# Joining two 256-column matmuls into one of 512 columns in seven-product (Strassen-type) layers of a diffusion block

## The chip, the cores and the metric

The kernel runs on one core of one Trainium2 chip. The metric is device time in microseconds (us) of one execution; lower is better. Five engines work side by side, each in the order of its own queue: TensorE (PE in the profile; its weight loads are shown as PEld), VectorE (DVE), ScalarE (ACT), GpSimd (POOL) and SyncE (SP). SP and POOL mainly issue DMAs here.

## The reference

One layer on 512 latent tokens of width 2048: modulated RMSNorm, attention and short-conv mixer, output projection, then a gated MLP with a depthwise convolution over tokens. All arithmetic is float32. What the change touches is the MLP:

```python
def conv_ffn(h, w_up, cw, cb, w_down):
    u = dwconv3(h @ w_up, cw, cb)          # 2048 -> 2 x 5504
    a, g = jnp.split(u, 2, axis=-1)
    return (a * jax.nn.silu(g)) @ w_down   # 5504 -> 2048

# x = x + gt_f * conv_ffn(hf_l, ...), then a final RMSNorm
```

## The kernel before

Tensors lie with features on the 128 partitions and the 512 tokens (T) along the columns; `HS` are the two halves H0 and H1 of 256 tokens. To keep float32 accuracy with the reduced-precision matmul type, every operand is split into a high part (a cast, on ACT) and a low part (operand minus cast, on DVE). A product then takes three matmuls: high weights by high data, high weights by low data, low weights by high data. `mm3` issues these three; each of the three loads its own 128x128 weights.

The up projection: the first three output tiles (six column groups) go row by row (`row`, over the 16 input tiles `hf`). For the other 40 tiles f a 2x2 scheme with seven products takes the place of eight: token halves and weight blocks are added and subtracted beforehand (`t_sums` makes the token sums T1, T2 and T4; `up_load` brings blocks 11, 12, 22 and sums s1 and s3, the sums by a second DMA that adds onto the first). The products run in the order p1 ("11"), p2 ("21"), then of the tile before q4 ("4") and q3 ("22"), then p6 ("2"), q5 ("1") and p7 ("3"). Each (`product`) splits a 128x1024 weight block (`split4`: u19p2h is the high part for product p2 of tile 19, u19p2l the low part; three buffers each) and calls `mm3` for eight input tiles into 256 columns of a PSUM bank. `u19a`, `u19b` and `u19c` are the three banks of tile 19. The results are put together on DVE into `cg` and `ca`, and `acts` applies convolution and gating; L1213 and L1214 form the weight sums in place on DVE (u_11 plus s1; u_12 plus that).

The activations of the last 36 tiles are paired; `pair_sums` makes seven operands of 256 columns per pair, high and low halves side by side in one tile of 512 columns (`tp`), which POOL's DMAs send to DRAM (`t_d`). The work of `pair_sums` is a generator in the queue `bg`; each `pump(1)` runs it up to its next `yield`, and `product` pumps once per product. Tiles of the pool `t2` hold the `tp` operands, the `hf` and the `T` tiles.

The down projection does seven tiles plainly (`d`, 512 columns), then 24 steps of seven products over a window of six pairs: operands come back from DRAM (`w<-t_d`, in the same side-by-side form), `weights_of` loads the blocks of a step and forms s3 on DVE (L1290), after which POOL's DMA adds a fourth block onto s1 (L1291), and L1351 and L1352 add s1 onward. `seven` runs a product, `into` adds its result onto the accumulators `c` (L1338 in steps 8 and later). `v19q4l` is the low part of the weights for product q4 of step 19. From step 16 on sums of squares for the final norm (`ssq`, L347) run on DVE too.

The order of instructions on each engine is set by a scheduler when the program is built, from the code's order and its own time estimates; the engines then run their queues in that order.

Of the kernel before, what the change touches and what calls it, by code (L numbers as in the profile page):

```python
# [72 lines left out]
def block_kernel(ctx, tc, xt, ctxt, ctxn, c, c_ctx, w_ada, small, w_in, w_inc, w_q, w_kv, w_out,  # L73
# [65 lines left out]
    nth = {"raw": 0, "w": 0}  # L139
# [45 lines left out]
    def mm3(ps, w, x, first, last, on_top=False):  # L185
        with tc.issue_after(behind.pop()) if behind else ExitStack():
            PE.matmul(ps, w[0], x[0], start=first, stop=False, skip_group_check=on_top)  # L187
        PE.matmul(ps, w[0], x[1], start=False, stop=False, skip_group_check=on_top)  # L188
        PE.matmul(ps, w[1], x[0], start=False, stop=last, skip_group_check=on_top)  # L189

# [740 lines left out]
    def hf_tile(j, cols=slice(0, T)):  # L931
        if j not in hf:
# [7 lines left out]
        hi, lo = (z[:, cols] for z in hf[j])  # L940
        A.copy(out=hi, in_=xr)
        ins = V.tensor_tensor(out=lo, in0=xr, in1=hi.bitcast(F32), op=ALU.subtract)
        hf_last[:] = hf_last[1], ins.ins
# [91 lines left out]
    def pair_sums(p, e, o):  # L1035
# [4 lines left out]
        def put(n, src):  # L1040
            z = t2([P, T], F32R, f"tp{p}{n}")
            A.copy(out=z[:, :256], in_=src)  # L1042
            V.tensor_tensor(out=z[:, 256:], in0=src, in1=z[:, :256].bitcast(F32), op=ALU.subtract)  # L1043
            G_.dma_start(t_d[p, OPS.index(n)], z.bitcast(F32))  # L1044
# [30 lines left out]
    def t_sums(j):  # L1075

        e, o = xres[2 * j], xres[2 * j + 1]
        i, c = j // 2, HS[j % 2]
        if j % 2 == 0:
            for n in (1, 2, 4):  # L1080
                TT[n, i] = tuple(t2([P, T], F32R, f"T{n}{i}{z}") for z in "hl")

        def put(dst, src):
            hi, lo = dst
            A.copy(out=hi, in_=src)
            V.tensor_tensor(out=lo, in0=src, in1=hi.bitcast(F32), op=ALU.subtract)

        V.tensor_tensor(out=e[:, H0], in0=e[:, H0], in1=e[:, H1], op=ALU.subtract)
        V.tensor_tensor(out=e[:, H1], in0=o[:, H1], in1=e[:, H1], op=ALU.subtract)
        put(half_of(hf[2 * j], 1), e[:, H1])  # L1090
        V.scalar_tensor_tensor(out=o[:, H1], in0=e[:, H0], scalar=-1.0, in1=o[:, H1], op0=ALU.mult, op1=ALU.subtract)
        V.scalar_tensor_tensor(out=o[:, H0], in0=o[:, H1], scalar=-1.0, in1=o[:, H0], op0=ALU.mult, op1=ALU.subtract)
        for n, src in ((1, e[:, H0]), (2, o[:, H1]), (4, o[:, H0])):
            put(tuple(z[:, c] for z in TT[n, i]), src)

    def operand(n, j):
        if n in ("11", "3"):
            return half_of(hf[2 * j], n == "3")
        if n in ("21", "22"):
            return half_of(hf[2 * j + 1], n == "22")  # L1100
        return half_of(TT[int(n), j // 2], j % 2)
# [21 lines left out]

    pss = [bank_of(i, f"uf{g}") for g, i in enumerate((2, 3, 4, 5, 1, 0))]
# [3 lines left out]
    for k in range(EARLY):  # L1128
        row(pss, held[k], hf[k], k, H0)
        pump(1)  # L1130
    drain()
    for k in range(EARLY):
        hf_tile(k, H1)
        row(pss, held[k], hf[k], k, H1)
# [12 lines left out]
    for k in range(EARLY, NK):  # L1147
# [7 lines left out]
        row(pss, w, hf[k], k)  # L1155
# [21 lines left out]
    def finish(st):  # L1177
        f, a22, s4, u2, u3, pa, pc, cg, ca = st
        product(pa, a22, "4", f"u{f}q4", False)
        A.activation(ca[:, H0], pa[:, :256], AF.Identity, scale=-1.0)  # L1180
        product(pc, s4, "22", f"u{f}q3", False)
        V.tensor_tensor(out=cg[:, H1], in0=pc[:, :256], in1=u2, op=ALU.add)  # L1182
        acts(f, cg, ca)
# [15 lines left out]
    for f in range(G // 2, NF):  # L1199
# [8 lines left out]
        ca = cp.tile([P, T], F32, tag="ca", bufs=2, name=f"ca{f}")  # L1208
# [3 lines left out]
        V.tensor_tensor(out=cg[:, H0], in0=pb[:, :256], in1=u1, op=ALU.add)  # L1212
        V.tensor_tensor(out=a11, in0=a11, in1=s1, op=ALU.add)  # L1213
# [105 lines left out]
    def seven(z, ps, a, n, nm, first, pump_at=()):  # L1319
# [11 lines left out]
    def into(z, i, cols, ps, minus=False):  # L1331

        o = acc2[z.m + i][:, cols]
        if z.st < 8:
            ins = V.tensor_tensor(out=o, in0=o, in1=ps[:, :256], op=ALU.subtract if minus else ALU.add)
        else:
            g = ng[:, z.m + i:z.m + i + 1] if minus else mod[:, 80 + z.m + i:81 + z.m + i]
            ins = V.scalar_tensor_tensor(out=o, in0=ps[:, :256], scalar=g, in1=o, op0=ALU.mult, op1=ALU.add)  # L1338
# [255 lines left out]
```

## Time and profile before

| | |
|---|---|
| runs | 2155.0, 2151.49, 2147.65 us; median 2151.49 |
| profiled execution | 2158.83 us, span 2157.0 us, clock 0.994 |
| up projection, seven products | about 884 to 1695 us of the span |
| plain part of down | about 1697 to 1770 us |
| 24 steps of down | about 1770 to 2145 us |

The columns of the views: in the timeline, start, duration, engine, line, operation, output<-inputs, partitions x elements, and in brackets the idle time before the instruction with what ended it. Durations overlap a little: an engine starts its next instruction before the last one's end, so the distance between starts is what a queue of instructions costs. In the table of windows each engine has its busy time and its number of instructions.

### The profile page before, as it was taken

The page shows a single profiled execution, that of the slowest core. Times are in us where ns is not written, and L with a number is a line of the kernel's source. Part 1 is how long each engine was busy: PE and PEld are TensorE (multiplying, and loading weights), DVE is VectorE, ACT ScalarE, POOL GpSimd, SP SyncE. Part 2 cuts the span into 40 slices and gives each one's busy share as a digit, 9 for nine tenths or more (in the row PEclk, how much of TensorE's full clock was granted, in tenths as well). Part 3 has the DMA queues.
Part 4 walks back from the last instruction along what each step waited for, and adds up shares of the span by engine and source line. Part 5 has one row for each costly group of instructions (what it writes and reads, how often), then busy time and mean ns, then how long its engine had stood idle before and what let it go on. Part 6 is the DMA issues. An engine that isn't in the chain of part 4 may idle for free.

```text
span 2157.0 us, 37744 instructions
## 1 busy us (share of the span) xinstructions
PE 2104.9 (98%) x14458; PEld 1946.7 (90%) x14458; DVE 1769.0 (82%) x2859; ACT 1047.1 (49%) x1710; POOL 188.1 (9%) x270
## 2 busy tenths in 40 slices
PE   7899999999999999999999999999999999999997
PEld 4688788888888888999999999999999889999997
DVE  7998987778886889788888788788888658888877
ACT  5533333555552237555555555555555333333445
POOL 0000000000000000111211111111111000000000
PEclk9999999999999999999999999999999999999998
DMA  9979785334559986577887877877887999877683
GB/s 335 345 275 337 270 279 176 128 126 162 177 199 348 344 278 192 159 217 201 241 232 215 240 229 220 237 231 219 241 229 218 341 335 290 254 220 236 196 247 111
DMA packets 162121, 513.89 MB, mean 238 GB/s; under 512 B 18962, under 2 KB 23314, under 8 KB 156306
## 3 DMA queue, kind: packets, MB, share of 16 engines
q1 hardware_dynamic: 133364, 418.14, 56.5%
q0 software_dynamic: 27488, 92.29, 18.3%
q8 instruction: 113, 1.85, 0.3%
q10 hardware_dynamic: 1088, 1.05, 0.1%
q14 instruction: 68, 0.56, 0.1%
HBM read 464.22 MB, written 46.14 MB: 237 GB/s over the span
## 4 chain that ended last, share of the span: by engine, by line
PE 86%; DVE 6%; DMA 5%; issue 1%; ACT 1%; SPq 0%; DVEq 0%; POOLq 0%; ACTq 0%
PE pp L187 4%; PE pp L189 4%; PE pp L188 4%; PE o L189 1%; PE o L187 1%; PE o L188 1%; DMA ada<-in_w_ada 1%; PE d L187 1%; PE d L189 1%; PE d L188 1%; PE uf L187 1%; PE uf L188 1%; PE of L187 1%; PE of L188 1%; PE of L189 1%
## 5 line engine op out<-in xcount | busy, mean ns | idle before, releaser
L1044 POOL DMA_DIRECT2D t_d<-tp x126 | 71.9, 574 | 468.3 <-DVE tp L1043 465.4
L255 DVE SCALAR_TENSOR_TENSOR ada<-ada,sv 128x1024 f32<-128x1024 f32 x68 | 82.1, 1219 | 12.1 <-DMA ada<-in_w_ada 12.0
L166 ACT CAST w_0h<-rw 128x512 fp32r<-128x512 f32 (+1 forms) x63 | 38.3, 618 | 108.3 <-PE pp L188 63.1
L1121 POOL DMA_DIRECT2D u_s<-in_w_up x80 | 70.2, 878 | 224.4 <-DMA u_s<-in_w_up 131.5
L233 DVE SCALAR_TENSOR_TENSOR ada<-ada,sv 128x1024 f32<-128x1024 f32 x64 | 77.5, 1217 | 4.4 <-DMA ada<-in_w_ada 3.9
L522 DVE SCALAR_TENSOR_TENSOR ada<-ada,svc 128x1024 f32<-128x1024 f32 x64 | 76.0, 1220 | 2.3 <-DMA ada<-in_w_ada 2.3
L785 POOL TENSOR_TENSOR gr<-gr,half 128x8 f32<-128x8 f32 x4 | 10.1, 2524 | 628.7 <-DVE gr L784 536.8
L1042 ACT CAST tp<-a 128x256 fp32r<-128x256 f32 x90 | 34.7, 405 | 60.5 <-DMA t_d<-tp 54.1
L167 DVE TENSOR_TENSOR w_0l<-rw,w_0h 128x512 fp32r<-128x512 f32 (+1 forms) x63 | 42.6, 681 | 22.3 <-ACT w_0h L166 22.3
L255 DVE SCALAR_TENSOR_TENSOR ra<-ra,sv 128x1024 f32<-128x1024 f32 x44 | 52.5, 1217 | 1.1 <-DMA ra<-in_w_ada 1.1
L1213 DVE TENSOR_TENSOR u<-u,u_s 128x1024 f32<-128x1024 f32 x40 | 48.8, 1219 | 0.7 <-DMA u_s<-in_w_up 0.7
L1214 DVE TENSOR_TENSOR u<-u,u 128x1024 f32<-128x1024 f32 x40 | 48.7, 1218 | 0.0
L1043 DVE TENSOR_TENSOR tp<-a,tp 128x256 fp32r<-128x256 f32 x90 | 36.2, 418 | 12.3 <-ACT tp L1042 12.3
L756 ACT CAST pth<-t 128x384 fp32r<-128x384 f32 x64 | 28.6, 485 | 26.4 <-PE t L753 26.4
L1042 ACT CAST tp<-ts 128x256 fp32r<-128x256 f32 x36 | 14.6, 407 | 43.5 <-DMA t_d<-tp 41.1
L533 DVE TENSOR_TENSOR acc<-acc,pp 128x512 f32<-128x512 f32 x50 | 34.0, 680 | 2.1 <-PE pp L189 2.1
L757 DVE TENSOR_TENSOR ptl<-t,pth 128x384 fp32r<-128x384 f32 x64 | 33.2, 549 | 2.7 <-ACT pth L756 2.7
L737 DVE TENSOR_REDUCE mn<-s 128x1 f32<-128x768 f32 x32 | 30.4, 952 | 4.8 <-PE s L726 4.6
L1043 DVE TENSOR_TENSOR tp<-ts,tp 128x256 fp32r<-128x256 f32 x36 | 15.2, 421 | 23.3 <-ACT tp L1042 23.3
L1005 ACT ACTIVATE g<-cg,sm 128x512 f32<-128x512 f32 x40 | 32.5, 813 | 0.5 <-DVE cg L1182 0.5
L1005 ACT ACTIVATE a<-ca,sm 128x512 f32<-128x512 f32 x40 | 32.1, 803 | 0.0
L1013 ACT ACTIVATE g<-g 128x512 f32<-128x512 f32 x43 | 27.2, 632 | 6.4 <-DVE g L1007 6.4
(15967 smaller groups left out, 9398.2 us busy)
## 6 DMA issues: line engine op xcount, KB each, us to landing
ada<-in_w_ada SPq DMA_DIRECT2D x196, 512.0 KB, 6.0
u<-in_w_up SPq DMA_DIRECT2D x120, 512.0 KB, 8.2
w<-t_d SPq DMA_DIRECT2D x161, 256.0 KB, 5.2
u_s<-in_w_up SPq DMA_DIRECT2D x80, 512.0 KB, 4.3
u_s<-in_w_up POOLq DMA_DIRECT2D x80, 512.0 KB, 8.9
t_d<-tp POOLq DMA_DIRECT2D x126, 256.0 KB, 4.9
v<-in_w_dnw SPq DMA_DIRECT2D x72, 384.0 KB, 5.4
ra<-in_w_ada SPq DMA_DIRECT2D x22, 1024.0 KB, 4.9
```

The lines of the kernel that those rows point to most:

```text
L187: PE.matmul(ps, w[0], x[0], start=first, stop=False, skip_group_check=on_top)
L188: PE.matmul(ps, w[0], x[1], start=False, stop=False, skip_group_check=on_top)
L189: PE.matmul(ps, w[1], x[0], start=False, stop=last, skip_group_check=on_top)
L233: V.scalar_tensor_tensor(out=r, in0=r, scalar=1.0, in1=vec[:, i * 1024:(i + 1) * 1024], op0=ALU.mult, op1=ALU.mult, accum_out=col[:, i:i + 1])
L255: keep(V.scalar_tensor_tensor(out=r, in0=r, scalar=1.0, in1=svs[i], op0=ALU.mult, op1=ALU.mult, accum_out=lc[:, t % 4:t % 4 + 1] if i else ...
L522: keep(V.scalar_tensor_tensor(out=raw[q], in0=raw[q], scalar=1.0, in1=svc[:, q * 1024:(q + 1) * 1024], op0=ALU.mult, op1=ALU.mult, accum_o ...
L1005: A.activation(u, src, AF.Identity, bias=s("fb", m), scale=s("fw", 86 + m))
L1042: A.copy(out=z[:, :256], in_=src)
L1043: V.tensor_tensor(out=z[:, 256:], in0=src, in1=z[:, :256].bitcast(F32), op=ALU.subtract)
L1044: G_.dma_start(t_d[p, OPS.index(n)], z.bitcast(F32))
L1121: G_.dma_start(r[-1], src[more], accum_op=ALU.add)
L1213: V.tensor_tensor(out=a11, in0=a11, in1=s1, op=ALU.add)
```

## The change

In the products "21", "1", "4" and "22" of the up tiles, and in "21", "1" and "22" of down's steps 8 to 21, the two matmuls with the same high weights become one of 512 columns, whose operand has the high and the low half side by side (`mm2`). The low half's result then lies in columns 256 to 511 of the bank, and a further DVE instruction adds it (`beside` in up, a second pass of the loop in `into` in down). To have such operands, the odd `hf` tiles and all `T` tiles are stored as high half beside low half of one token half; the row-wise part at the start (`up_row`) then works on the odd tiles by halves, with six matmuls of 256 columns where three of 512 stood. `product` pumps on every second product, every third `tp` tile comes from a buffer of its own (`tq`), `ca` has one buffer instead of two, and the cast of `tp` is put behind the last cast of `split4` on ACT.

```diff
+    def mm2(ps, w, x, first, last, on_top=False):
+        n = x.shape[1] // 2
+        with tc.issue_after(behind.pop()) if behind else ExitStack():
+            PE.matmul(ps[:, :2 * n], w[0], x, start=first, stop=False, skip_group_check=on_top)
+        PE.matmul(ps[:, :n], w[1], x[:, :n], start=False, stop=last, skip_group_check=on_top)
...
+    def side_by_side(z, src):
+        n = T // 2
+        A.copy(out=z[:, :n], in_=src)
+        return V.tensor_tensor(out=z[:, n:], in0=src, in1=z[:, :n].bitcast(F32), op=ALU.subtract)
...
         def put(n, src):
-            z = t2([P, T], F32R, f"tp{p}{n}")
-            A.copy(out=z[:, :256], in_=src)
+            nth["tp"] += 1
+            if nth["tp"] % 3 or p == PAIRS - 1:
+                z = t2([P, T], F32R, f"tp{p}{n}")
+            else:
+                z = cp.tile([P, T], F32R, tag="tq", bufs=1, name=f"tp{p}{n}")
+            with tc.issue_after(last_hi[0]):
+                A.copy(out=z[:, :256], in_=src)
...
+    def up_row(w, k, hs=(0, 1)):
+        if k % 2 == 0:
+            row(pss, w, hf[k], k, slice(hs[0] * 256, hs[-1] * 256 + 256))
+            return
+        for g in range(G):
+            for h in hs:
+                mm3(pss[g][:, HS[h]], w[g], two(hf[k, h]), False, k == NK - 1 and h == 1)
...
+    APART = ("21", "1", "4", "22")
+
+    def beside(dst, ps, minus=False):
+        V.tensor_tensor(out=dst, in0=dst, in1=ps[:, 256:], op=ALU.subtract if minus else ALU.add)
...
         for j in range(8):
-            mm3(ps[:, :256], part(w, j), operand(n, j), first and j == 0, j == 7, on_top=not first)
-        pump(1)
+            x = operand(n, j)
+            if n in APART:
+                mm2(ps, part(w, j), x, first and j == 0, j == 7, on_top=not first)
+            else:
+                mm3(ps[:, :256], part(w, j), x if isinstance(x, tuple) else two(x), first and j == 0, j == 7, on_top=not first)
+        nth["up"] += 1
+        pump(nth["up"] % 2)
...
+        z.apart = 8 <= st < STEPS - 2
...
-            mm3(ps[:, :256], part(w, j), (x[:, :256], x[:, 256:]), first and j == 0, j == WIN - 1, on_top=not first)
+            if z.apart and n in APART[:2] + APART[3:]:
+                mm2(ps, part(w, j), win[n, p], first and j == 0, j == WIN - 1, on_top=not first)
+            else:
+                mm3(ps[:, :256], part(w, j), two(win[n, p]), first and j == 0, j == WIN - 1, on_top=not first)
...
-        if z.st < 8:
-            ins = V.tensor_tensor(out=o, in0=o, in1=ps[:, :256], op=ALU.subtract if minus else ALU.add)
-        else:
-            g = ng[:, z.m + i:z.m + i + 1] if minus else mod[:, 80 + z.m + i:81 + z.m + i]
-            ins = V.scalar_tensor_tensor(out=o, in0=ps[:, :256], scalar=g, in1=o, op0=ALU.mult, op1=ALU.add)
+        for x in (ps[:, :256], ps[:, 256:])[:2 if z.apart and ps is not z.pa else 1]:
+            if z.st < 8:
+                ins = V.tensor_tensor(out=o, in0=o, in1=x, op=ALU.subtract if minus else ALU.add)
+            else:
+                g = ng[:, z.m + i:z.m + i + 1] if minus else mod[:, 80 + z.m + i:81 + z.m + i]
+                ins = V.scalar_tensor_tensor(out=o, in0=x, scalar=g, in1=o, op0=ALU.mult, op1=ALU.add)
```

How the instructions stand on the engines, at three places. Lines of the changed kernel have other numbers (L1213 is L1265 there, L999 is L1024, L1338 is L1397, L1351 is L1410).

TensorE, up, product p2 of tile 19 (bank u19b), before:

```order
L187 MATMUL u19b_12352<-hf1h_7571,u19p2h_12386 128x256
L188 MATMUL u19b_12352<-hf1l_7572,u19p2h_12386 128x256
L189 MATMUL u19b_12352<-hf1h_7571,u19p2l_12387 128x256
L187 MATMUL u19b_12352<-hf3h_7673,u19p2h_12386 128x256
L188 MATMUL u19b_12352<-hf3l_7674,u19p2h_12386 128x256
L189 MATMUL u19b_12352<-hf3h_7673,u19p2l_12387 128x256
```

and the same place now:

```order
L196 MATMUL u19b_12009<-hf10_7575,u19p2h_12046 128x512
L197 MATMUL u19b_12009<-hf10_7575,u19p2l_12047 128x256
L196 MATMUL u19b_12009<-hf30_7676,u19p2h_12046 128x512
L197 MATMUL u19b_12009<-hf30_7676,u19p2l_12047 128x256
L196 MATMUL u19b_12009<-hf50_7691,u19p2h_12046 128x512
```

Sixteen matmuls and weight loads do what twenty-four did, over the same number of columns.

VectorE, up, between the sums of the weights of tile 20 and the low part for q3 of tile 19, before:

```order
L1213 TENSOR_TENSOR u20_11_12339<-u20_11_12339,u20_s1_12343 128x1024
L1015 TENSOR_TENSOR a18_12480<-a18_12480,g18_12475 128x512
L999 TENSOR_TENSOR u20p2l_12641<-u20_12_12341,u20p2h_12640 128x1024
L1051 TENSOR_TENSOR a17_12245<-a18_12480,a17_12245 128x256
L1056 SCALAR_TENSOR_TENSOR ts5_12513<-ts5_12513,a18_12480 128x256
L1214 TENSOR_TENSOR u20_12_12341<-u20_12_12341,u20_11_12339 128x1024
L999 TENSOR_TENSOR u19q4l_12677<-u19_22_12096,u19q4h_12676 128x1024
L1224 SCALAR_TENSOR_TENSOR ca19_12355<-u19c_12353,u193_12586 128x256
L1043 TENSOR_TENSOR tp53_12582<-a17_12245,tp53_12582 128x256
L1043 TENSOR_TENSOR tp522_12634<-a18_12480,tp522_12634 128x256
L999 TENSOR_TENSOR u19q3l_12710<-u19_12_12088,u19q3h_12709 128x1024
```

and now:

```order
L1265 TENSOR_TENSOR u20_11_11996<-u20_11_11996,u20_s1_12000 128x1024
L1024 TENSOR_TENSOR u20p2l_12269<-u20_12_11998,u20p2h_12268 128x1024
L1040 TENSOR_TENSOR a18_12124<-a18_12124,g18_12119 128x512
L1266 TENSOR_TENSOR u20_12_11998<-u20_12_11998,u20_11_11996 128x1024
L1024 TENSOR_TENSOR u19q4l_12298<-u19_22_11785,u19q4h_12297 128x1024
L1277 SCALAR_TENSOR_TENSOR ca19_12219<-u19c_12010,u193_12217 128x256
L1083 TENSOR_TENSOR a17_11903<-a18_12124,a17_11903 128x256
L1088 SCALAR_TENSOR_TENSOR ts5_12157<-ts5_12157,a18_12124 128x256
L1024 TENSOR_TENSOR u19q3l_12320<-u19_12_11777,u19q3h_12319 128x1024
L1075 TENSOR_TENSOR tp522_12339<-a18_12124,tp522_12339 128x256
L1207 TENSOR_TENSOR ca19_12219<-ca19_12219,u19c_12010 128x256
```

The low part for p2 now stands right behind the sum L1265, one instruction sits between it and the low part for q4 besides L1266, and the pair's pieces stand behind q4 and q3; L1207 is `beside`, four times per tile.

VectorE, down, step 20, from the sum that waits for POOL's DMA on, before (a row for s3 of step 21 follows in both):

```order
L1351 TENSOR_TENSOR v2011_22731<-v2011_22731,v20s1_22732 128x768
L1338 SCALAR_TENSOR_TENSOR c4_18805<-v18c_22547,mod_90,c4_18805 128x256
L999 TENSOR_TENSOR v20p2l_22968<-v2012_22733,v20p2h_22967 128x768
L347 TENSOR_TENSOR ssq_18441<-ssq_18441,eq40_22897 128x512
L1338 SCALAR_TENSOR_TENSOR c7_18811<-v19a_22742,gn_95,c7_18811 128x256
L1352 TENSOR_TENSOR v2012_22733<-v2012_22733,v2011_22731 128x768
L347 TENSOR_TENSOR ssq_18441<-ssq_18441,eq50_22900 128x512
L999 TENSOR_TENSOR v19q4l_22995<-v1922_22538,v19q4h_22994 128x768
L1338 SCALAR_TENSOR_TENSOR c8_19120<-v20a_22939,mod_90,c8_19120 128x256
L999 TENSOR_TENSOR v20p6l_23020<-v2011_22731,v20p6h_23019 128x768
L1338 SCALAR_TENSOR_TENSOR c8_19120<-v20b_22940,mod_90,c8_19120 128x256
L999 TENSOR_TENSOR v20q5l_23045<-v20s1_22732,v20q5h_23044 128x768
```

and now:

```order
L1410 TENSOR_TENSOR v2011_21551<-v2011_21551,v20s1_21552 128x768
L1397 SCALAR_TENSOR_TENSOR c4_17780<-v18c_21382,mod_90,c4_17780 128x256
L1024 TENSOR_TENSOR v20p2l_21773<-v2012_21553,v20p2h_21772 128x768
L1397 SCALAR_TENSOR_TENSOR c4_17780<-v18c_21382,mod_90,c4_17780 128x256
L1397 SCALAR_TENSOR_TENSOR c7_17786<-v19a_21562,gn_95,c7_17786 128x256
L1411 TENSOR_TENSOR v2012_21553<-v2012_21553,v2011_21551 128x768
L1024 TENSOR_TENSOR v19q4l_21795<-v1922_21373,v19q4h_21794 128x768
L355 TENSOR_TENSOR ssq_17416<-ssq_17416,eq40_21702 128x512
L1397 SCALAR_TENSOR_TENSOR c8_18100<-v20a_21744,mod_90,c8_18100 128x256
L1024 TENSOR_TENSOR v20p6l_21820<-v2011_21551,v20p6h_21819 128x768
L355 TENSOR_TENSOR ssq_17416<-ssq_17416,eq50_21705 128x512
L1397 SCALAR_TENSOR_TENSOR c8_18100<-v20b_21745,mod_90,c8_18100 128x256
```

One more addition (the second c4) stands between the sum and the end of the stretch, the low part for q4 stands ahead of both sums of squares, and s3 of the next step comes after q5's low part as before.

More of the change, by code (lines that the diff above doesn't have):

```diff
@@ L926, in block_kernel, with two @@
     hf = {}
+    def side_by_side(z, src):
+        n = T // 2
+        A.copy(out=z[:, :n], in_=src)
+        return V.tensor_tensor(out=z[:, n:], in0=src, in1=z[:, :n].bitcast(F32), op=ALU.subtract)
+    def two(z):
+        return z[:, :T // 2], z[:, T // 2:]
     hf_last = [None, None]
     def hf_tile(j, cols=slice(0, T)):
-        if j not in hf:
+        if j % 2 == 0 and j not in hf:
             hf[j] = tuple(t2([P, T], F32R, f"hf{j}{z}") for z in "hl")
@@ L939, in hf_tile @@
         A.activation(xr, xr, AF.Identity, bias=mod[:, 48 + j:49 + j], scale=sc)
-        hi, lo = (z[:, cols] for z in hf[j])
-        A.copy(out=hi, in_=xr)
-        ins = V.tensor_tensor(out=lo, in0=xr, in1=hi.bitcast(F32), op=ALU.subtract)
+        if j % 2 == 0:
+            hi, lo = (z[:, cols] for z in hf[j])
+            A.copy(out=hi, in_=xr)
+            ins = V.tensor_tensor(out=lo, in0=xr, in1=hi.bitcast(F32), op=ALU.subtract)
+        else:
+            for h in range(2):
+                if cols in (HS[h], slice(0, T)):
+                    hf[j, h] = t2([P, T], F32R, f"hf{j}{h}")
+                    ins = side_by_side(hf[j, h], xres[j][:, HS[h]])
         hf_last[:] = hf_last[1], ins.ins
@@ L1077, in t_sums @@
         e, o = xres[2 * j], xres[2 * j + 1]
[L1078 to L1081, printed above, removed]
+        for n in (1, 2, 4):
+            TT[n, j] = t2([P, T], F32R, f"T{n}{j}")
         def put(dst, src):
@@ L1093, in t_sums @@
         for n, src in ((1, e[:, H0]), (2, o[:, H1]), (4, o[:, H0])):
-            put(tuple(z[:, c] for z in TT[n, i]), src)
+            put(two(TT[n, j]), src)
     def operand(n, j):
@@ L1128, in block_kernel @@
     for k in range(EARLY):
-        row(pss, held[k], hf[k], k, H0)
+        up_row(held[k], k, (0,))
         pump(1)
@@ L1133, in block_kernel @@
         hf_tile(k, H1)
-        row(pss, held[k], hf[k], k, H1)
+        up_row(held[k], k, (1,))
         pump(1)
@@ L1154, in block_kernel @@
             nxt = prepare(k + 1)
-        row(pss, w, hf[k], k)
+        up_row(w, k)
         if k % 2:
@@ L1212, in block_kernel @@
         V.tensor_tensor(out=cg[:, H0], in0=pb[:, :256], in1=u1, op=ALU.add)
+        beside(cg[:, H0], pb)
         V.tensor_tensor(out=a11, in0=a11, in1=s1, op=ALU.add)
@@ L1223, in block_kernel @@
         u3 = aside(pa, f"u{f}3")
+        ca = cp.tile([P, T], F32, tag="ca", bufs=1, name=f"ca{f}")
         V.scalar_tensor_tensor(out=ca[:, H1], in0=pc[:, :256], scalar=-1.0, in1=u3, op0=ALU.mult, op1=ALU.subtract)
+        beside(ca[:, H1], pc, True)
         if first_acts:
```

11 lines of the change are left out of this document (6 added, 5 removed).

## Prediction

> **What bounds the kernel now.** I read the page's engine totals and the shares of its chain first, then the table of windows by stage.
>
> ```profile
> PE 2104.9 (98%) x14458; PEld 1946.7 (90%) x14458; DVE 1769.0 (82%) x2859; ACT 1047.1 (49%) x1710; POOL 188.1 (9%) x270
> PE 86%; DVE 6%; DMA 5%; issue 1%; ACT 1%; SPq 0%; DVEq 0%; POOLq 0%; ACTq 0%
> ...
> 780.00:884.00 104.00, 99.88 (x628) 90.29 (x627) 91.22 (x202) 62.38 (x124) 6.15 (x9) 0.98 0.65 199
> 884.00:1685.00 801.00, 801.00 (x6675) 800.91 (x6673) 664.49 (x879) 460.29 (x687) 140.20 (x209) 1.00 0.79 225
> 1697.00:1765.00 68.00, 68.00 (x294) 55.16 (x293) 35.39 (x67) 19.90 (x29) 4.96 (x8) 1.00 0.99 358
> ```
>
> A window's row gives length, then busy time and instructions of PE, weight loads, DVE, ACT and POOL, then granted clock, DMA share and GB/s. From 884 to 1685 (the 40 up tiles of seven products) PE is busy for all of 801.00 us: no data is ever late. DVE has 664.49 (83%). On the chain PE has 86%. A gain there must come from the spacing of the matmuls, and a loss from DVE or a transfer becoming late.
>
> 801.00/6675 = 120.0 ns from one 256-column matmul to the next. For 512 columns, the first and last rows that overlap the plain stage of down, 294 in all:
>
> ```profile
> 1696.74 0.39 PE L187 MATMUL d<-yl0h,dw00h 128*128 128x512 f32 x1
> ...
> 1764.82 0.40 PE L188 MATMUL d<-yl6l,dw16h 128*128 128x512 f32 x1
> ```
>
> (1764.82 − 1696.74)/293 = 232.4 ns. Twice 256 costs 240.0. Whether a mixed sequence keeps this is seen in the attention stage, where both widths alternate:
>
> ```profile
> 513.13 0.28 PE L725 MATMUL s<-krc,qst 128*128 128x256 f32 x1
> 513.25 0.40 PE L187 MATMUL pkl<-kl0h,wk2h 128*128 128x512 f32 x1
> ...
> 514.41 0.40 PE L189 MATMUL pkl<-kl1h,wk2l 128*128 128x512 f32 x1
> 514.64 0.28 PE L726 MATMUL s<-krc,qst 128*128 128x256 f32 x1
> ```
>
> A 512 follows a 256 after 0.12 us, a 256 follows a 512 after 0.23: each costs what it costs among its own kind.
>
> **The change on TensorE.** Three matmuls of 256 columns take 3 × 120.0 = 360.0 ns; joined, 232.4 + 120.0 = 352.4. A triple saves 7.6 ns.
> - Up: 40 tiles × 4 products × 8 = 1280 triples, −9.7 us. A tile goes from 7 × 8 × 360 ns = 20.16 us to 4 × 8 × 352.4 + 3 × 8 × 360 = 19.92.
> - Odd rows at the start (k = 7 to 15, six groups each): 30 times six of 256 for three of 512, 720.0 − 697.2 = 22.8 ns, +0.7 us.
> - Down, steps 8 to 18: 11 × 3 products × 6 = 198 triples, −1.5 us. Steps 19 to 21 are below.
>
> The page "TensorE: Matmul & The Clock Gate" of the Trainium skill (section "Wait — 56ns, not 53.3ns?") weighs against this: it gives start to start as N/2.4 GHz plus about 2.5 ns per matmul, so joining would save 2.5 ns. The trace differs: 2 × 120.0 − 232.4 = 7.6 ns. By the page the sum below would be −2.9 us (an estimate); I go by the trace.
>
> **VectorE in up.** Each tile gets four `beside` additions of 128x256 out of PSUM. The row nearest in form is the L1212 sum, 0.42 us long, followed after 0.33:
>
> ```profile
> 1189.60:1209.70 20.10, 17.26 (x24) 1.00 0.84 243
> 1209.70:1229.80 20.10, 16.35 (x21) 1.00 0.77 209
> ...
> 1203.67 1.22 DVE L999 TENSOR_TENSOR u18q4l<-u,u18q4h 128x1024 fp32r<-128x1024 f32 x1
> 1208.08 0.42 DVE L1212 TENSOR_TENSOR cg<-u19b,u 128x256 f32<-128x256 f32 x1
> 1208.41 1.22 DVE L999 TENSOR_TENSOR u19p6l<-u,u19p6h 128x1024 fp32r<-128x1024 f32 x1
> 1211.06 1.23 DVE L999 TENSOR_TENSOR u19q5l<-u_s,u19q5h 128x1024 fp32r<-128x1024 f32 x1 [1.44 <-ACT u19q5h L998]
> 1212.98 0.42 DVE L1182 TENSOR_TENSOR cg<-u18c,u 128x256 f32<-128x256 f32 x1 [0.69 <-PE u18c L189]
> 1213.94 1.23 DVE L999 TENSOR_TENSOR u19p7l<-u_s,u19p7h 128x1024 fp32r<-128x1024 f32 x1 [0.54 <-ACT u19p7h L998]
> 1219.26 1.23 DVE L1213 TENSOR_TENSOR u<-u,u_s 128x1024 f32<-128x1024 f32 x1 [0.31 <-DMA u_s<-in_w_up]
> ```
>
> The first two rows are DVE alone in one tile with pieces of a pair and in the next, without. Four additions cost 4 × 0.33 to 4 × 0.42, that is 1.3 to 1.7 us. The mean, 664.49/801 × 20.16 = 16.7 us, becomes about 18.2 of 19.92 (91%). The heavy tile here had 17.26 of 20.10 without a stall of PE; spreading the pair's pieces over more products removes such peaks. So DVE fits, if its idle time shrinks. In the rows here that idle time ends on casts, a bank and a transfer (1.44, 0.69, 0.54, 0.31: 2.98 us, most of the second tile's 20.10 − 16.35). These are waits of an engine that runs ahead; where it runs later, they end sooner. What a delay meets first is the lead of the low parts over TensorE:
>
> ```profile
> 1202.20 1.22 DVE L999 TENSOR_TENSOR u19p2l<-u,u19p2h 128x1024 fp32r<-128x1024 f32 x1
> 1204.38 0.28 PE L189 MATMUL u19b<-hf1h,u19p2l 128*128 128x256 f32 x1
> ...
> 1219.02 0.28 PE L189 MATMUL u19a<-hf0h,u19p7l 128*128 128x256 f32 x1
> ```
>
> u19p2l ends at 1203.42, used at 1204.38 (0.96 us); u19p7l ends at 1215.17, used at 1219.02 (3.85 us). A single addition of 0.42 ahead of a low part fits into either. I take 0; the upper bound is that none of the 2.98 shrinks: 18.2 + 3.0 − 19.9 = 1.3 us a tile, +52 us over 40 tiles.
>
> Behind a late `beside` stands the next product on top of the same bank: q3 on q5's, with four products (11.4 us) between them; 0. `ca` with one buffer makes its first write wait for the last read by `acts`, which DVE itself passes earlier in its own order; 0. Five odd `hf` tiles cost one more DVE instruction each, 5 × 0.42 = 2.1 us at most; DVE has 91.22 of the 104.00 us before 884, and the trace shows no wait of the row products for it there; 0, bound +2.1.
>
> **ScalarE and the third tile.** Casts of the pair's operands waited for their buffer:
>
> ```profile
> L1042 ACT CAST tp<-a 128x256 fp32r<-128x256 f32 x90 | 34.7, 405 | 60.5 <-DMA t_d<-tp 54.1
> L1042 ACT CAST tp<-ts 128x256 fp32r<-128x256 f32 x36 | 14.6, 407 | 43.5 <-DMA t_d<-tp 41.1
> ```
>
> 95.2 us of ACT's queue, with the casts of weights behind them. The third buffer and the pump on every second product should remove most of it. It is worth 0, since TensorE waited for nothing there; it pays for part of the new load on DVE. The same edit moves the DMAs to `t_d` past the weights' sums in POOL's queue, next.
>
> **The weights' loop in up.** The sums come by a chain that feeds itself: the low part for q4 frees the block, SP loads s1, POOL adds the second block onto it, L1213 uses it, and the next q4 follows.
>
> ```profile
> u_s<-in_w_up SPq DMA_DIRECT2D x80, 512.0 KB, 4.3
> u_s<-in_w_up POOLq DMA_DIRECT2D x80, 512.0 KB, 8.9
> ...
> 1209.33 0.89 POOL L1121 DMA_DIRECT2D u_s<-in_w_up  x1 [1.28 <-DMA u_s<-in_w_up]
> 1223.95 1.22 DVE L999 TENSOR_TENSOR u19q4l<-u,u19q4h 128x1024 fp32r<-128x1024 f32 x1
> ```
>
> u18q4l ends at 1204.89, POOL starts its sum at 1209.33 (4.4 us), L1213 begins at 1219.26 (9.9), and u19q4l ends at 1225.17 (5.9): 20.2, as long as the tile. Now L1213 and q4's low part have fewer pieces between them (about 5.4 us by the order, pieces at these durations): 4.4 + 9.9 + 5.4 = 19.7 against 19.92. Margin 0.2; taken 0. POOL's row shows what can spend it: it issues the pair's DMAs to `t_d` in the same queue, 0.89 us for an issue, and those now come evenly over the products, so that one may stand ahead of the sum in more tiles than before. One such issue that is not ready on time would cost its wait; on the average over 40 tiles I bound this by 0.1 beyond the margin, +4 us, and below by 0, since a faster loop cannot help TensorE, which waits for nothing.
>
> **Down.** Step 11's sum, step 19's and 20's, with s3 of the next step and its DMA between:
>
> ```profile
> 1931.43 0.96 DVE L1351 TENSOR_TENSOR v<-v,v11s 128x768 f32<-128x768 f32 x1 [0.81 <-DMA v11s<-in_w_dnw]
> 1937.18 0.96 DVE L1290 TENSOR_TENSOR v12s<-v,v12s 128x768 f32<-128x768 f32 x1
> ...
> 2052.64 0.96 DVE L1351 TENSOR_TENSOR v<-v,v19s 128x768 f32<-128x768 f32 x1 [1.06 <-DMA v19s<-in_w_dnw]
> ...
> 2058.11 0.47 DVE L1338 SCALAR_TENSOR_TENSOR c<-v19a,mod,c 128x256 f32<-128x256 f32 x1
> 2058.51 0.94 DVE L999 TENSOR_TENSOR v19p6l<-v,v19p6h 128x768 fp32r<-128x768 f32 x1
> ...
> 2060.64 0.95 DVE L1290 TENSOR_TENSOR v20s<-v,v20s 128x768 f32<-128x768 f32 x1
> 2069.21 0.96 DVE L1351 TENSOR_TENSOR v<-v,v20s 128x768 f32<-128x768 f32 x1 [2.51 <-DMA v20s<-in_w_dnw]
> ...
> 2062.11 7.00 DMA v20s<-in_w_dnw
> ...
> PE v19a L189 <- DVE v19q4l L999: 0.9, 1, 0.9
> PE v20a L189 <- DVE v20q4l L999: 0.9, 1, 0.9
> PE v22b L189 <- DVE v22p2l L999: 0.5, 1, 0.5
> ```
>
> A step takes TensorE 7 × 6 × 360 ns = 15.12 us. In step 11 the loop from the sum to s3's end is 6.71; with a DMA of 7.00 and the 0.5 or so of its issue it closes in 14.2. Two of the three more additions per step (0.40 each, from 2058.11 to 2058.51) can stand in that stretch: 15.0, against 15.12 − 3 × 6 × 7.6 ns = 14.98. That is level, and DVE has idle time there (0.81 ahead of step 11's sum), so I take 0, with 0.1 × 11 = +1.1 as the bound. From 2052.64 to 2069.21 the loop takes 16.57 us, longer than 15.12: in steps 19 to 21 it sets the pace, and TensorE's saving there (0.4) is not counted. One more addition stands inside that loop in steps 19 and 20 each, 2 × 0.40: +0.8. Bounds are 0 (what TensorE waits for, v19a's and v20a's row, is the low part for q4, and that now goes ahead of a sum of squares) and +1.6 (two additions in the loop).
>
> **Sum.** −9.7 + 0.7 − 1.5 + 0.8 = −9.7 us on the profiled execution: 2158.83 → 2149.1. It lies 7.3 above the median; carried to the median, 2151.49 − 9.7 = 2141.8.
>
> **Rivals.**
> - The weights' loop or a late low part in up eats part: the margin of 0.2 speaks for it, TensorE's full 801.00 against. At 0.1 us per tile 4.0 of the 9.7 go, at 0.24 (the tile back at 20.16) all of up's gain: 2146 to 2151.5.
> - VectorE becomes the bound, and the kernel is slower. Place: the low parts p2 and p6, whose leads are shortest. It decides once work plus in-order waits exceed 19.92 us: 18.2 + 1.7 of the 2.98. If 2.5 of it stay, 20.7 a tile, 0.78 over, +31 − 9.7: 2173; slower than before by 0.3% it is from 20.3. For it: 91% busy, and no tile of before had 18.2. Against it: from the light tile to the heavy one DVE's idle time fell from 3.75 to 2.84, by all of the 0.91 that the work rose, without a stall, so the waits do give way.
> - The fixed cost per matmul in these products is smaller than 7.6 ns, since the widths alternate without pause and the same weights are loaded less often: at a third of it, 2.5 ns, −3.2 + 0.2 − 0.5 + 0.8 = −2.7, 2148.8. The rows at 513 us speak against it. (This is the skill's 2.5 ns above.)
> - Down's additions cost more: if all 42 at 0.4 (three products, 14 steps) reached the path, +16.8 − 9.7: 2158.6. Against it, steps 8 to 18 have idle time of DVE before the sum (0.81 in step 11); of them at most 3 steps are near: +3, 2145.
>
> **Chances.** Forecast, within 3 us (2138.5 to 2144.8): 0.62. Loop or lateness in up, 2146 to 2151.5: 0.17. Smaller fixed cost: 0.06. Down: 0.05. VectorE as the bound: 0.10. A difference of 0.3% (6.5 us) is about what a measurement of this kernel can tell, so faster means below 2145.0: 0.62 and a part of the fourth case, 0.64; slower means above 2158, nearly all of the last, 0.09; the rest 0.27. The range 2138.0 to 2151.5 leaves out the last case, and some above its end.
>
> **What the profile after would show.** Right: in products p2, q4, q3 and q5 starts alternating 0.23 and 0.12 us apart, 2.82 us a product; tiles of 19.92; still no wait of TensorE from 884 on; DVE at about 91% there, its waits shorter; ACT's waits for `t_d` nearly gone; waits of v19a and v20a for q4's low part within 0.5 us of 0.9. Wrong: waits of TensorE for low parts in up, tiles above 20, L1265 (before L1213) waiting 1 us or more for `u_s`, or a pair of matmuls that takes 0.357 us in place of 0.352, v20's sum later than 17 us after v19's.

## The result: slower, and the profile after

The changed kernel takes 2165.0 us (median of six runs, 2159.64 to 2172.31) against 2150.97 (2147.65 to 2155.52) before: ratio 1.0066, 95% interval 1.0046 to 1.0087. Forecast were 2141.8 and a range of 2138.0 to 2151.5. The change costs 14 us where 9.7 were to be gained.

The page of after, engine totals and the shares of the chain; then its windows (columns as before):

```profile
PE 2096.4 (97%) x13016; PEld 1873.2 (87%) x13016; DVE 1839.1 (85%) x3066; ACT 1045.6 (48%) x1715; POOL 187.9 (9%) x270
PE 77%; DMA 11%; DVE 8%; issue 2%; ACT 2%; POOL 0%; SPq 0%; DVEq 0%; POOLq 0%; ACTq 0%
...
884.00:1685.00 801.00, 784.14 (x5341) 727.86 (x5340) 707.92 (x1019) 450.39 (x675) 138.29 (x206) 0.99 0.77 221
```

1442 matmuls fewer, as counted. But TensorE, busy for all of the 801.00 us before, now idles for 16.9 of them (801.00 − 784.14), and DMA holds 11% of the chain instead of 5%. The waits of TensorE by what they waited for (total, times, longest):

```profile
PE u30a L187 <- ACT u L1224: 4.4, 1, 4.4
PE u24a L187 <- ACT u L1224: 3.7, 1, 3.7
...
PE u10a L187 <- ACT u L1224: 2.4, 1, 2.4
PE u18a L187 <- ACT u L1224: 2.2, 1, 2.2
PE u36a L187 <- ACT u L1224: 2.1, 1, 2.1
PE u12a L187 <- ACT u L1224: 2.0, 1, 2.0
```

L1224 is `aside`: ACT copies bank a after product p6, and p7, which adds onto the same bank, must wait for the copy. No low part of DVE is in the list, none of the weights' sums either. The stall of tile 24, in the timelines of ACT, POOL and PE:

```profile
1309.50 0.71 ACT L1074 CAST tp<-a 128x256 fp32r<-128x256 f32 x2 [1.57 <-DVE a L1083]
1313.23 0.40 ACT L1074 CAST tp<-ts 128x256 fp32r<-128x256 f32 x1
1317.93 1.05 ACT L1023 CAST u25p1h<-u 128x1024 fp32r<-128x1024 f32 x1
1323.94 0.40 ACT L1074 CAST tp<-a 128x256 fp32r<-128x256 f32 x1 [4.97 <-DMA t_d<-tp]
1324.26 0.37 ACT L1224 COPY u<-u24a 128x256 f32<-128x256 f32 x1
...
1313.29 0.87 POOL L1151 DMA_DIRECT2D u_s<-in_w_up  x1 [14.29 <-DMA u_s<-in_w_up]
1313.86 1.39 POOL L1076 DMA_DIRECT2D t_d<-tp  x2
...
1320.72 0.28 PE L188 MATMUL u25a<-hf0l,u25p1h 128*128 128x256 f32 x1
1324.67 0.58 PE L187 MATMUL u24a<-hf0h,u24p7h 128*128 128x256 f32 x1 [3.68 <-ACT u L1224]
1325.05 0.41 PE L188 MATMUL u24a<-hf0l,u24p7h 128*128 128x256 f32 x1
1325.27 0.41 PE L189 MATMUL u24a<-hf0h,u24p7l 128*128 128x256 f32 x1
```

Read it from the end. p7 starts at 1324.67, after 3.68 us idle, because the copy ran at 1324.26. Ahead of the copy in ACT's queue stands a cast of `tp`, which waited 4.97 us for a free buffer. The high parts of three operands had been cast into the buffers between 1309.50 and 1313.6, and two of the transfers that empty them stood on POOL behind L1151, which had been waiting 14.29 us for the first half of a weight sum (that half was on its way only from 1308.83 on, after q4's low part of tile 23 had freed its block at 1308.80); they were issued at 1313.86 and landed some 10 us later (10.4 us median from issue to landing, 1310 to 1326).

And the matmuls after the wait come 0.21 us apart, not 0.12. The windows of PE alone show why (granted clock behind the count):

```profile
1310.00:1318.00 8.00, 8.00 (x55) 1.00 0.68 188
1322.00:1326.00 4.00, 1.32 (x6) 0.67 1.06 324
1326.00:1330.00 4.00, 4.00 (x21) 0.50 0.57 188
1330.00:1334.00 4.00, 4.00 (x31) 0.98 0.16 28
```

The clock was halved for some 5 us, so 3.68 us of waiting made the tile 26.17 − 19.77 = 6.4 us longer. Tile 30's 4.41 made 7.3, tile 18's 2.21 (clock 0.57 from 1200 to 1204) 3.9; after 2.42 in tile 10 the clock stayed at 1.00 and the tile lost 2.7. The page "TensorE: Matmul & The Clock Gate" of the Trainium skill (section "What's actually happening") puts the drop to half rate after an idle window of about 3.4 us: the 3.68 and the 4.41 agree, the 2.21 does not.

Undisturbed tiles take 19.77 us, less than the 19.92 forecast: after, u21 and u22 start here.

```profile
1241.52 0.27 PE L187 MATMUL u21a<-hf0h,u21p1h 128*128 128x256 f32 x1
1261.29 0.27 PE L187 MATMUL u22a<-hf0h,u22p1h 128*128 128x256 f32 x1
```

### The profile page after: what moved, and what is told of

Read it like the earlier page. It is cut to its first block, busy times and chain, and to the rows that moved or that the text cites. A ratio compares the mean times of both kernels' runs of the same rounds, so it can differ in the third digit from the quotient of the medians.

```text
span 2162.6 us, 34970 instructions
## 1 busy us (share of the span) xinstructions
PE 2096.4 (97%) x13016; PEld 1873.2 (87%) x13016; DVE 1839.1 (85%) x3066; ACT 1045.6 (48%) x1715; POOL 187.9 (9%) x270
## 3 DMA queue, kind: packets, MB, share of 16 engines
q0 software_dynamic: 27488, 92.29, 17.9%
## 4 chain that ended last, share of the span: by engine, by line
PE 77%; DMA 11%; DVE 8%; issue 2%; ACT 2%; POOL 0%; SPq 0%; DVEq 0%; POOLq 0%; ACTq 0%
DMA t_d<-tp 4%; PE pp L187 4%; DMA u_s<-in_w_up 4%; PE pp L189 4%; PE pp L188 4%; PE o L188 1%; PE o L187 1%; PE o L189 1%; PE d L187 1%; PE d L188 1%; PE d L189 1%; DMA ada<-in_w_ada 1%; PE uf L187 1%; PE uf L188 1%; PE of L187 1%
## 5 line engine op out<-in xcount | busy, mean ns | idle before, releaser
L1076 POOL DMA_DIRECT2D t_d<-tp x126 | 81.4, 659 | 438.8 <-DVE tp L1075 426.3
L1151 POOL DMA_DIRECT2D u_s<-in_w_up x80 | 70.5, 881 | 278.2 <-DMA u_s<-in_w_up 217.3
L1074 ACT CAST tp<-a 128x256 fp32r<-128x256 f32 x90 | 35.9, 406 | 74.3 <-DMA t_d<-tp 57.4
L1265 DVE TENSOR_TENSOR u<-u,u_s 128x1024 f32<-128x1024 f32 x40 | 48.9, 1222 | 7.7 <-DMA u_s<-in_w_up 7.6
L1266 DVE TENSOR_TENSOR u<-u,u 128x1024 f32<-128x1024 f32 x40 | 48.8, 1220 | 0.0
L1038 ACT ACTIVATE g<-g 128x512 f32<-128x512 f32 x43 | 27.2, 632 | 15.2 <-DVE g L1032 14.8
L748 ACT ACTIVATE p<-s,mn 128x768 f32<-128x768 f32 x32 | 29.3, 915 | 1.6 <-DVE mn L745 1.3
L1032 DVE SCALAR_TENSOR_TENSOR a<-ca,sm,a 128x511 f32<-128x511 f32 x40 | 29.9, 747 | 0.0
```

What stands on the lines that cost most here:

```text
L1151: G_.dma_start(r[-1], src[more], accum_op=ALU.add)
L1266: V.tensor_tensor(out=a12, in0=a12, in1=a11, op=ALU.add)
```

## The experiments

By stage, each from its profile: "up" runs from the first matmul of tile u3 to that of u42, "8 to 18" from the first of down's step 8 to that of step 19, "end" from there to the end of v23c. Medians and intervals are of runs beside the kernel before on the same chip.

| kernel | median, us | ratio to before, interval | up | 8 to 18 | end |
|---|---|---|---|---|---|
| before | 2150.97 | | 777.6 | 166.3 | 90.7 |
| changed | 2165.0 | 1.0066 (1.0046 to 1.0087) | 788.3 | 164.0 | 89.0 |
| behind_copy | 2136.71 | 0.9929 (0.9914 to 0.9945) | 762.8 | 164.0 | 88.4 |
| spread_only | 2170.5 | 1.0085 (1.0066 to 1.0105) | 790.4 | 164.5 | 88.0 |
| join_no_spread | 2214.37 | 1.0274 (1.0255 to 1.0294) | 832.1 | 164.0 | 92.9 |
| before_again | 2155.4 (one run) | | 777.6 | 165.4 | 88.0 |
| behind_no_join | 2142.7 | 0.9959 (0.9944 to 0.9974) | 769.0 | 164.5 | 87.2 |
| layout_only | 2145.49 | 0.9971 (0.9957 to 0.9984) | 769.0 | 164.5 | 88.5 |
| no_behind | 2218.5 | 1.0313 (1.0296 to 1.0329) | 845.0 | 164.0 | 89.8 |
| behind_copy_up | 2140.51 | 0.994 (0.992 to 0.9959) | 762.8 | 164.5 | 89.1 |
| behind_copy_two | 2225.37 | 1.0332 (1.0312 to 1.0353) | 848.1 | 164.0 | 91.7 |
| before_nudge | 2147.12 | 0.9979 (0.9962 to 0.9997) | 769.1 | 165.0 | 88.2 |
| td_on_sp | 2144.69 | 0.9967 (0.995 to 0.9985) | 767.1 | 164.0 | 88.5 |

Theory A: the stalls are the cast that waits for `t_d` ahead of the copy. Theory B: they are DVE's 160 more additions in up.

**behind_copy.** The cast moved behind the copy, and the `pump` with it, so the scheduler's order changes on DVE too:

```diff
-        nth["up"] += 1
-        pump(nth["up"] % 2)
+        if n not in ("11", "2", "3"):
+            nth["up"] += 1
+            pump(nth["up"] % 2)
     def aside(ps, nm):
         r = cp.tile([P, 256], F32, tag="uu", bufs=4, name=nm)
-        A.copy(out=r, in_=ps[:, :256])
+        ins = A.copy(out=r, in_=ps[:, :256])
+        last_hi[0] = ins.ins
+        nth["up"] += 1
+        pump(nth["up"] % 2)
```

> The changed kernel, but in up the queue of a pair's work is pumped after the copy of the bank (aside) where a product has one, and the cast of tp is issued behind that copy and no longer only behind the last cast of split4. Theory A (the cast that waits for t_d stands ahead of the copy on ACT, and p7 waits for the copy): no wait of TensorE for the copy above 0.3 us in up, every tile at 19.77 us, about -15.5 us in up and -2.5 in down against before: 2133. Theory B (four more additions per tile make VectorE late, the place of the cast matters little): TensorE waits again, for low parts or copies, in sum 10 us or more, 2145 to 2165.

2136.71, 3.7 above theory A's 2133, with no wait of TensorE in up's tiles at all, and every tile from u8 on at 19.77. The window of the stage, and the group of casts on the page (busy, mean, idle before and its cause):

```profile
884.00:1685.00 801.00, 799.98 (x5475) 742.18 (x5475) 724.44 (x1047) 467.09 (x695) 141.05 (x210) 1.00 0.82 233
...
L1074 ACT CAST tp<-a 128x256 fp32r<-128x256 f32 x90 | 36.4, 405 | 14.5 <-DMA t_d<-tp 14.4
```

DVE does all its additions here, 724.44 of 801 us (90%), and TensorE does not wait. Theory B falls; so does the prediction's rival of DVE as the bound. This kernel is faster than before (by 0.7%) and than the changed one.

**spread_only.** Nothing joined, no additions, the rest of the change kept:

```diff
-            if n in APART:
+            if n in JOIN:        # JOIN = (); beside() does nothing
-        z.apart = 8 <= st < STEPS - 2
+        z.apart = False
```

> The changed kernel with three matmuls of 256 columns everywhere in up's seven products and in down, and without the added additions: what is left is the third tp tile, the pump on every second product, the cast behind split4's last cast, one ca buffer, and the stored form of the operands. Theory A: TensorE waits for the copy in some of the tiles as in the changed kernel, 5 to 25 us in all, 2155 to 2175 (its tiles take 20.16). Theory B: no such wait, 2148 to 2154.

2170.5: slower than the changed kernel, with nothing joined. Eleven waits for the copy of 1.0 to 2.0 us, 17.0 in all:

```profile
PE u34a L187 <- ACT u L1226: 2.0, 1, 2.0
...
PE u10a L187 <- ACT u L1226: 1.0, 1, 1.0
```

So these stalls come with the moved casts and need no joining. (What joining does to the pair's work as it was before is the next run.)

**join_no_spread.** Joined, with the pair's work as before:

```diff
-            if nth["tp"] % 3 or p == PAIRS - 1:
+            if True:
-            with tc.issue_after(last_hi[0]):
-                A.copy(out=z[:, :256], in_=src)
+            A.copy(out=z[:, :256], in_=src)
-        pump(nth["up"] % 2)
+        pump(1)
```

and two `ca` buffers.

> The changed kernel with the joined matmuls and their additions, but the pair's work as before: two tp tiles from the common pool, a pump on every product, the cast where the scheduler puts it, two ca buffers. Theory A: no wait of TensorE for the copy, tiles at 19.77, 2133 to 2138; ACT waits for t_d as before (some 95 us). Theory B: TensorE waits for what VectorE makes, in most tiles with pieces of a pair, above 2150.

2214.37, which theory A did not expect; the time is in theory B's range, but what TensorE waits for is not DVE's. No wait for the copy, but fifteen of 2.1 to 4.0 us for the high parts of p1, which ACT casts.

```profile
PE u13a L187 <- ACT u13p1h L1023: 4.0, 1, 4.0
PE u27a L187 <- ACT u27p1h L1023: 3.7, 1, 3.7
...
1298.52 0.40 ACT L1073 CAST tp<-a 128x256 fp32r<-128x256 f32 x1 [4.20 <-DMA t_d<-tp]
1298.83 1.04 ACT L1023 CAST u23p1h<-u 128x1024 fp32r<-128x1024 f32 x1
```

The same wait for `t_d` now stands ahead of the cast of p1's weights. Theory A has to be put wider: what is lost is decided by which of ACT's instructions stands behind the waiting cast, and how soon TensorE needs it. In the kernel before, the waiting casts of tiles 18 and 19 stood ahead of the weights of q5, of `g` and the weights of p2, and of the weights of q3:

```profile
1189.58 0.41 ACT L1042 CAST tp<-ts 128x256 fp32r<-128x256 f32 x1 [1.53 <-DMA t_d<-tp]
1189.89 1.05 ACT L998 CAST u18q5h<-u_s 128x1024 fp32r<-128x1024 f32 x1
...
1196.54 0.36 ACT L1174 COPY u<-u18a 128x256 f32<-128x256 f32 x1
1199.68 0.41 ACT L1042 CAST tp<-a 128x256 fp32r<-128x256 f32 x1 [2.78 <-DMA t_d<-tp]
1199.99 0.63 ACT L1013 ACTIVATE g<-g 128x512 f32<-128x512 f32 x1
1200.52 1.04 ACT L998 CAST u19p2h<-u 128x1024 fp32r<-128x1024 f32 x1
...
1204.64 0.41 ACT L1042 CAST tp<-a 128x256 fp32r<-128x256 f32 x1 [1.74 <-DMA t_d<-tp]
...
1205.57 1.05 ACT L998 CAST u18q3h<-u 128x1024 fp32r<-128x1024 f32 x1
```

TensorE took up these three weights 4.6, 2.6 and 3.3 us after their casts had ended, so the waits cost nothing. The weights of p1 have the least in hand: in the trace of before their cast ends at most 1.75 us ahead of TensorE, those of the other products 4.4 to 4.9 us (medians of tiles 7 to 41). The kernel layout_only, further down, has the same pair's work without joining; there, too, no waiting cast stands directly ahead of p1's weights, and TensorE does not wait. So in join_no_spread the joined code got another order on ACT from the scheduler, with fifteen waiting casts ahead of p1's weights, 57.4 us of waiting. Whether DVE's additions also make the transfers later was not separated.

**no_behind.** The changed kernel without the one line:

```diff
-            with tc.issue_after(last_hi[0]):
-                A.copy(out=z[:, :256], in_=src)
+            A.copy(out=z[:, :256], in_=src)
```

> The changed kernel without the one line that puts the cast of tp behind the last cast of split4. The scheduler then places most casts ahead of p7's weights, some ahead of p1's. Theory A: no wait of TensorE for the copy, tiles mostly at 19.77; waits of a weights' cast at most in a few tiles: 2134 to 2145. If instead the third tile and the slower pump make the stalls wherever the cast stands: TensorE waits 15 us or more, for p1's or p7's high parts, 2155 or more.

2218.5, against theory A's 2134 to 2145: without the line another cast of the pair stands ahead of p1's weights, or ahead of the two activations in front of them, and waits up to 6.77 us; fifteen waits of TensorE of 2.1 to 5.1 us, all for p1's high parts. Time and waits are those of the other case put forward, but its reason, that third tile and slower pump stall wherever the cast stands, does not hold: behind_copy has both and no stall.

```profile
1339.30 0.40 ACT L1073 CAST tp<-a 128x256 fp32r<-128x256 f32 x1 [4.70 <-DMA t_d<-tp]
1339.61 1.04 ACT L1023 CAST u25p1h<-u 128x1024 fp32r<-128x1024 f32 x1
```

The line that put the cast ahead of the copy saves 53 us against leaving it out, and costs 28 against putting it behind the copy.

**behind_copy_two.** Behind the copy, but without the third tile and with a pump after every product (`if True:` in place of the test on `nth["tp"]`, `pump(1)`, two `ca` buffers).

> The kernel of behind_copy without the third tp tile: all tp operands in the common pool's two free tiles, a pump after every product, two ca buffers; the cast still stands behind the copy. Theory A in its present form (a cast's wait for t_d costs what TensorE needs soon from ACT behind it, wherever that is): ACT still waits 80 us or more for t_d, but now with the casts of q4, q3, p6 or p2 behind it, which have some 2 to 3 us in hand: stalls of 0 to 1.5 us in some tiles, 2137 to 2160. If the place behind the copy is enough by itself: 2136 to 2138. If VectorE's load made the stalls: no different from join_no_spread, above 2200.

2225.37; the waits are again for p1's weights (sixteen, 2.8 to 4.8 us). The casts wait longer and in other places:

```profile
L1074 ACT CAST tp<-ts 128x256 fp32r<-128x256 f32 x36 | 14.6, 406 | 78.2 <-DMA t_d<-tp 74.4
```

The place behind the copy is not enough by itself. The time is in the range of the third case, but TensorE waits for ACT's casts and not for VectorE, so none of the three gives the reason: with two tiles a cast of `ts` waits for its buffer ahead of two activations and p1's weights (sixteen times). The place does its work only together with the third tile and the slower pump; which of these two it takes was not run apart.

**td_on_sp.** The cause of the wait itself, with ACT's order as in the changed kernel:

```diff
-            G_.dma_start(t_d[p, OPS.index(n)], z.bitcast(F32))
+            SP.dma_start(t_d[p, OPS.index(n)], z.bitcast(F32))
```

> The changed kernel with one word changed: the transfers of tp to t_d are issued by SP's queue and not by POOL's; ACT's order is the same, the cast stands ahead of the copy as in the changed kernel. If the long waits of the cast come from POOL's queue, where a t_d stands behind a u_s that waits some 14 us for its first half: the casts wait below 20 us in all (57 there), TensorE's waits for the copy nearly vanish (below 3 us), 2136 to 2145. If the transfer itself is too slow for three tiles, or SP's queue holds it as long: waits as before, 2155 to 2165.

2144.69. No wait for the copy is left, and none of the casts' long waits is for `t_d`:

```profile
L1074 ACT CAST tp<-a 128x256 fp32r<-128x256 f32 x90 | 35.8, 404 | 38.9 <-DVE a L1093 20.2
...
PE u41b L197 <- DVE u41p2l L1024: 0.5, 1, 0.5
PE u31b L197 <- DVE u31p2l L1024: 0.4, 1, 0.4
```

One word takes the chain away at its root, POOL's queue, with nearly the same order on ACT. What remains, up at 767.1 and not 762.8, goes with later weight sums: L1265 waits 39.7 us for `u_s` here (7.6 in the changed kernel), and in some tiles from 28 on TensorE waits 0.1 to 0.5 us for low parts of p2 and q4.

**What joining is worth: behind_no_join, layout_only, before_nudge.** Undisturbed tiles of spread_only took 19.94 us with every matmul at 256 columns, not 20.16. Three kernels separate this: behind_copy with nothing joined (the edits of spread_only on it); before with only the new storage of operands (spread_only and join_no_spread together); and before with one matmul more:

```diff
         w = split4(a, 1024, nm)
+        if nm == f"u{G // 2}p1":
+            PE.matmul(ps[:, :128], part(w, 0)[0], operand(n, 0)[0][:, :128], start=True, stop=True, skip_group_check=True)
```

> The kernel of behind_copy (cast of tp behind the copy) with three matmuls of 256 columns in place of the joined pairs, in up and down, without the added additions. Tells what joining alone is worth. Theory A (the stalls come from the cast ahead of the copy): no wait of TensorE for the copy. On the pitch: if the spacing of 256-column matmuls goes with the stored form of the operands, tiles take 19.94 us as the clean ones of spread_only, 2143, and joining is worth 6 to 7 us; if it is a matter of chance or of the joined form, tiles take 20.16, 2151, and joining 15.

> The kernel before with the new form of the odd hf tiles and of the T tiles (high half beside low half) and the row part that goes with it, nothing joined, the pair's work as before. If the stored form sets the spacing of 256-column matmuls: tiles of 19.94, 2142 to 2144. If not: tiles of 20.16, 2151 to 2153. Theory A: the cast that waits for t_d stands ahead of the weights' casts as before, no wait of TensorE for the copy, unless shorter tiles use up the lead.

> The kernel before with one extra matmul of 128 columns (overwritten at once) ahead of the first seven-product tile, u3. Tells whether the spacing of 120.0 or 118.67 ns is a phase into which TensorE falls at the start of a stretch and stays until it waits. If so, tiles may change to 19.93 (2143 to 2145) by this alone; if the spacing goes with the stored form of the operands: 20.16, 2152.

2142.7, 2145.49 and 2147.12, up 769.0, 769.0 and 769.1. The window of the stage in layout_only, and the first matmuls of u21 and u22 in before_nudge:

```profile
884.00:1685.00 801.00, 799.98 (x6727) 799.14 (x6726) 667.92 (x884) 466.19 (x694) 140.66 (x210) 1.00 0.80 229
...
1233.76 0.28 PE L187 MATMUL u21a<-hf0h,u21p1h 128*128 128x256 f32 x1
1253.70 0.28 PE L187 MATMUL u22a<-hf0h,u22p1h 128*128 128x256 f32 x1
```

6727 matmuls where 6675 stood; a tile of 19.94 us instead of 20.16. With one extra matmul at the head of the stage the spacing of the 6700 behind it was 118.7 ns and not 120.0. So the shorter spacing needs neither the stored form nor the joining: a stretch of matmuls runs in one of two rhythms, and in up each kernel kept its own through the stage; in spread_only the tiles came back to 19.94 us after each of eleven waits. In before, starts alternate by 118, 120 and 122 ns in a pattern of three; in the others by a pattern of five with one step of 115. The change alters the stretch ahead (six matmuls of 256 for three of 512), and all ten kernels with the new storage had the shorter rhythm from tile 5 on. That the extra matmul is the cause rests on one profile against two of before, and the median of before_nudge is only 4.5 us lower (0.6 to 8.2) where its stage is 8.5 shorter; what sets the rhythm stays open.

So of up's 777.6 − 762.8 = 14.8 us, 8.6 are the rhythm (777.6 to 769.0) and 6.2 the joining (behind_no_join to behind_copy): 5.0 ns for each of the 1232 triples between the two marks (39 × 32 = 1248, less the 16 of q4 and q3, which no tile ahead of u3 has), not 7.6. By medians joining is worth 2142.7 − 2136.71 = 6.0 us, measured on two chips.

**before_again.** The kernel before, unchanged.

> The kernel before, unchanged, for a second profile: shows how much its stages move from one execution to the next. All theories: 2147 to 2157, no wait of TensorE in up's tiles of seven products.

Up the same to the tenth; down's steps from 10 on at 14.95 us where the first profile had 15.12: there the same program shows both rhythms. So a difference of 2 us between two profiles in down says nothing.

**behind_copy_up.** behind_copy with `z.apart = False`, joined in up alone.

> The kernel of behind_copy with joined pairs in up alone; down's steps 8 to 21 have three matmuls of 256 columns and no added additions. From the stages of behind_copy and behind_no_join: joining saves 0.5 us in steps 8 to 18 and costs 1.2 in the last steps, so this one should be 0.7 us below behind_copy: 2136.0. If joining in down is worth its 2 us by count: 2138.7.

2140.51 (2134.19 to 2142.44) lies above behind_copy, not below, and neither of the two figures hit; its last steps took 89.1 us and those of behind_no_join, the same code from there on, 87.2. What joining in down costs or brings at the end stays open within these 2 us; in steps 8 to 18 it brings 0.5 (164.5 to 164.0). By medians joining in up alone would be worth 2142.7 − 2140.51 = 2.2 us where its stage is 6.2 shorter, so the medians do not resolve such amounts.

## Why the prediction was wrong

- **The step that failed** is "ScalarE and the third tile … It is worth 0, since TensorE waited for nothing there." Being idle for nothing *before* was the cover of an order in which the waiting cast had other work behind it. The edit moved that cast, and the prediction did not name what now stands behind it on ACT: the copy that p7 waits for. Cost in the profile: 788.3 − 762.8 = 25.5 us, of which 16.9 are waits; of the other 8.6, 7.3 lie in the three tiles whose clock was halved.
- It named the right queue with the wrong victim: "POOL's row shows what can spend it" asked what a `t_d` ahead of a weight sum costs the sum. What happened is the reverse, a `t_d` behind a sum that waits 14.29 us. The casts' waits for `t_d`, said to vanish, were still 57.4 us in L1074's group on `a` (54.1 before); only the 41.1 of the group on `ts` went, to nothing.
- The weights' loop held, but with less margin than the 0.2 taken: L1265 waited ten times for `u_s`, 7.6 us in 40 tiles and up to 1.6 (a sign of being wrong that the prediction had named), and 0.3 in behind_copy; TensorE waited for none of its products.
- DVE at "18.2 of 19.92" came close (90% of the stage in behind_copy, 17.9 of 19.77), and that its waits give way was right; the rival built on it gave the direction, slower, for a reason that behind_copy excludes.
- The sum for up, −9.7, stands against −14.8 in the undisturbed kernel, and it misses twice, in opposite directions. A fixed 7.6 ns per matmul was too much: 5.0 measured in up, and in steps 8 to 18, 0.5 us over 198 triples, 2.5. The other 8.6 of up's gain are the rhythm, for which the sum had no term: the 120.0 ns belonged to one of two rhythms, which the same stage's own row could not tell. Against 118.67 the same working gives 2 × 118.67 − 232.4 = 4.9. The rival with 2.5 ns was nearer in down; with it the terms add up to −2.7, as that rival has it, and the −2.9 given earlier leaves out the odd rows.
- The 0.7 us of the odd rows and the 0.8 in steps 19 and 20 are smaller than what two profiles of one kernel differ by; the waits for v19q4l and v21q4l went and that for v20q4l fell from 0.9 to 0.2, as one of the bounds had it, while the wait for v22p2l grew from 0.5 to 1.8.

The median moved by 14.0 us while the two profiles differ by 5.6 in span. The profile of before was taken in an execution of 2158.83, above all six runs timed beside the changed kernel; that one's profile, 2164.66, lies at its median.

## What to carry to other kernels

An instruction that waits costs what the instructions behind it in its queue make late, not the wait: when an edit moves one that waits, list the next two or three instructions on its engine and who needs them, also where the bounding engine waits for nothing today. A buffer that a DMA empties is as late as the queue that issues that DMA; look for the longest wait in that queue, not at the transfer's length. Before a gain of a few ns per instruction is multiplied by thousands, get the spacing from a second stretch or a second execution.

## What the runs showed of the hardware

- Two steady spacings of 256-column matmuls, each with its own weights: 120.0 and 118.67 ns at a granted clock of 1.00, kept for hundreds of us; 8.5 us of this kernel's up stage lie between them. With one more matmul of 128 columns at the start of the stretch the one profile taken had the shorter.
- A wait of TensorE can halve its clock for about 5 us (0.50 granted, 0.21 us between 256-column matmuls). In the five profiles with stalls in up (changed, spread_only, join_no_spread, no_behind, behind_copy_two) the granted clock stayed at 1.00 after all ten waits of 1.0 to 1.95 us, fell after six of the fourteen from 1.97 to 2.48 us (2.21 and one of 2.42 did it, another of 2.42 and 2.48 did not), and fell after all 39 from 2.72 to 5.14 us.
